# Second projection: VectorE and ScalarE kept in program order, and other PSUM banks for its first block

## The chip, the cores and the metric

The kernel runs on one core of a Trainium2 chip. The metric is the device time of one execution in microseconds. Five engines work beside each other, each through its own queue of instructions: TensorE (matmuls, PE in the profile, its weight loads PEld), VectorE (DVE), ScalarE (ACT), GpSimd (POOL) and SyncE (SP, which here issues nearly all loads).

## The reference

One layer of a decoder trunk on a sequence of 1024 rows of width 1024, everything in float32. What matters here is its end:

```
y_b = rms_norm(yz, ssm_norm_w ...)            # SSM branch, 2048 wide, normed in 8 groups
merged = sigmoid(g_a) * (y_a @ w_proj_a) + sigmoid(g_b) * (y_b @ w_proj_b)
x + gate * (merged @ w_out)                   # and a final rms_norm
```

`y_a @ w_proj_a` is called the first projection in this text, `y_b @ w_proj_b` the second, `merged @ w_out` the output product.

## The kernel before, in words

**Stages.** The kernel multiplies the normed input by a wide weight matrix, runs the SSD scan, and fills TensorE's gaps in the scan with the first projection (`proj_a`, eight blocks of 128 output columns, each accumulated in two PSUM banks, `pma`). L1308 empties those two banks with the gate applied and a store writes the result to DRAM. Then come the second projection (L1401 to L1647) and the output product (L1711 to L1778).

**Precision and operands.** A float32 product is made of three matmuls: an operand is split into a high part (a ScalarE cast, L1455, L1460, L1515, L1558) and a low part (a VectorE subtraction of the high part from the original, L1456, L1461, L1516, L1559), and high x high, high x low and low x high are added up in PSUM.

**The second projection.** It is a two-by-two product of blocks done with seven block products in place of eight (a Strassen form): p1, p5, p2, p3, p6, p7, p4 in this order. Each has eight steps `k`, numbered through as 56 units `u`. One step is twelve matmuls of 128x128 by 128x512, three into each of four PSUM banks (`multiply`, L1470). There are two sets of four banks: `psx` (tiles `x`), used by p1, p6, p7, p4, and `psy` (tiles `yp`), used by p5, p2, p3. p6, p7 and p4 add onto what p1 left in `psx`.

**What a step does.** In the loop at L1593, unit `u` issues its matmuls, then (`ahead`, L1570) the loads of unit u+6 (`loads`) and the operands of unit u+4 (`operands`, L1437). Operands are: for the four products that meet a fresh block of y, a norm on VectorE (`y_norm`, L1416); for p5, p6 and p7 a subtraction of blocks (L1447, L1449, L1452); the cast and the low part into rings of five slots (L1455, L1456); for p1 and p2 the cast and the low part of the weight block too (L1460, L1461); for p6 one more subtraction (L1463). In p1, two row sums of squares (`post2`, `post3`: TensorE, L1117 and L1131 on VectorE, L1121 on GpSimd, a store on ScalarE's queue) are finished for the last two groups of the norm. In the odd steps of p3, p7 and p4 a result is `merged` (L1521): gate times sum plus the other branch (L1527, L1528), and the sums that the output product needs (L1536 to L1542, and a split after a11). In p4 the splits of w_out begin (`BESIDE`). At the last step of a block its four banks are emptied: p1 and p5 by ScalarE copies (L1627, L1633), p2, p3, p6 and p7 by VectorE additions (L1630, L1637, L1640, L1643), p4 by `merged`.

**What sets the order.** The kernel is written in a layer that chooses the order of each engine's queue when it is compiled: it takes instructions by priority as a built-in model of the time says they are ready. `pin` (`keep_in_program_order`, L78) ties an instruction behind the one traced just before it on the same engine, so that it can't be moved ahead. `tc.high_priority()` lets an instruction be taken early. Before the change, all matmuls and all loads are pinned. On VectorE and ScalarE in the second projection only the splits of the first four units are, and the two L1308 of the last block of the first projection; the rest is ordered by the compiler's model. Each queue is then worked through in the order in which it was compiled.

**Banks.** `banks` (L1369) takes four PSUM banks for a set. Before, `psy` is taken first and so gets the lower four banks, `psx` the upper four.

Of the kernel before, what the change touches and what calls it, by code (L numbers as in the profile page):

```python
# [8 lines left out]
F32 = mybir.dt.float32  # L9
# [3 lines left out]
ALU = mybir.AluOpType  # L13
# [3 lines left out]
P = 128  # L17
# [18 lines left out]
def hybrid_kernel(  # L36
# [7 lines left out]
    V, A, G, PE = nc.vector, nc.scalar, nc.gpsimd, nc.tensor  # L44
# [33 lines left out]
    pin = tc.keep_in_program_order  # L78
# [7 lines left out]
    def f32(t):  # L86
        return t.bitcast(F32)
# [41 lines left out]
    snw = par2[:, 32:48]  # L129
# [38 lines left out]
    with tc.tile_pool(name="p0", bufs=1, reuse_waits="tile") as p0:  # L168
# [261 lines left out]
        sums = {(7, 5): [(last_sums, 0)], (7, 6): [(last_sums, 1)], (7, 8): [(last_sums, 2)]}  # L430
# [935 lines left out]
    room.extend(tag for k in range(KT - 2) for tag in ya_tags[k])  # L1366
    draw(left[0] - 5)

    def banks(name, c):  # L1369
        return [psb.tile([P, 512], F32, name=f"{name}{j}", tag=f"b{c}{j}") for j in range(4)]  # L1370

    big_r = [0]

# [30 lines left out]
    yt, rbs = {}, {}  # L1404
# [8 lines left out]

    def y_norm(n, h):
        t = yt[n, h]
        V.scalar_tensor_tensor(t, t, snw[:, n : n + 1], rbs[n // 2, h], op0=ALU.mult, op1=ALU.mult)  # L1416

    units = [(nm, k) for nm in ("p1", "p5", "p2", "p3", "p6", "p7", "p4") for k in range(KT)]
    aops, bops, raws = {}, {}, {}
# [17 lines left out]
    def operands(u):  # L1437

        nm, k = units[u]
        if nm in fresh:  # L1440
            n, h = fresh[nm]
            y_norm(n + k, h)
        b11, b12 = yt[k, 0], yt.get((k, 1))
        b21, b22 = yt.get((KT + k, 0)), yt.get((KT + k, 1))
        t = {"p1": b11, "p2": b21, "p5": b12, "p3": b22, "p6": b12, "p7": b11, "p4": b21}[nm]
        if nm == "p5":
            V.tensor_sub(b12, b12, b11)  # L1447
        elif nm == "p6":
            V.tensor_sub(b12, b22, b12)  # L1449
            give(f"yn{KT + k}_1")  # L1450
        elif nm == "p7":
            V.tensor_sub(b11, b12, b11)  # L1452
        hi, lo = turn(bh_r, f"{nm}bh{k}"), turn(bl_r, f"{nm}bl{k}")
        keep = pin if u < 4 else lambda i: i
        keep(A.copy(hi, t))  # L1455
        keep(V.tensor_sub(lo, t, f32(hi)))  # L1456
        bops[u] = hi, lo
        if nm not in WB:
            a, raw = aops[u], raws.pop(u)
            keep(A.copy(a[:, 0], raw))  # L1460
            keep(V.tensor_sub(a[:, 1], raw, f32(a[:, 0])))  # L1461
        if nm == "p6":
            V.tensor_sub(b21, b21, b12)  # L1463
        elif nm == "p7":
            give(f"yn{k}_0")
            give(f"yn{k}_1")
        elif nm == "p4":
            give(f"yn{KT + k}_0")

    def multiply(u, ps):  # L1470
        nm, k = units[u]
        first = nm in ("p1", "p5", "p2", "p3")
        a, (bh, bl) = aops.pop(u), bops.pop(u)
        for j in range(4):
            js = slice(j * P, (j + 1) * P)
            for n, (v, r) in enumerate(((0, bh), (0, bl), (1, bh))):
                pin(PE.matmul(ps[j], a[:, v, js], r, start=first and n + k == 0, stop=n == 2 and k == KT - 1,  # L1477
                              skip_group_check=not first))
# [30 lines left out]
    raw, opa, opb, freed = {}, {}, {}, {}  # L1509

    def split(nm, j, last=True):

        t, name = raw.pop((nm, j)) if last else raw[nm, j]
        hi, lo = place(f"{nm}h{j}"), place(f"{nm}l{j}")
        A.copy(hi[0], t)  # L1515
        V.tensor_sub(lo[0], t, f32(hi[0]))  # L1516
        opa[nm, j], freed[nm, j] = (hi[0], lo[0]), [hi, lo]
        if last and name:
            give(name)

    def merged(b, h, c, name):  # L1521


        th, ma = gates.pop((b, h))
        j, dst = b % 4, th if c is None else c
        acc = psx[j] if c is None else c
        V.scalar_tensor_tensor(dst, th, 1.0, acc, op0=ALU.add, op1=ALU.mult)  # L1527
        V.tensor_add(dst, dst, ma)  # L1528
        nm = (("a11", "a21"), ("a12", "a22"))[b // 4][h]
        raw[nm, j] = dst, name  # L1530
        if nm == "a11":
            split(nm, j, False)
        elif nm == "a21":
            raw["s3", j] = raw.pop(("a11", j))
            s3 = raw["s3", j][0]
            V.tensor_sub(s3, s3, dst)  # L1536
        elif nm == "a22":
            raw["s1", j] = raw.pop(("a21", j))
            s1, s3 = raw["s1", j][0], raw["s3", j][0]
            V.tensor_add(s1, s1, dst)  # L1540
            s2 = slot_tile(f"s2_{j}")
            V.tensor_sub(s2, dst, s3)  # L1542
            raw["s2", j] = s2, f"s2_{j}"

    def fourth(j):
        s4 = slot_tile(f"s4_{j}")
        V.tensor_sub(s4, raw["a12", j][0], raw["s2", j][0])
        raw["s4", j] = s4, f"s4_{j}"

    wor = {}  # L1550
# [4 lines left out]

    def wo_split(nm, j):
        hi, t = place(f"wh{nm}{j}"), wor.pop((nm, j))
        A.copy(hi[0], f32(t))  # L1558
        V.tensor_sub(t, f32(t), f32(hi[0]))  # L1559
        opb[nm, j] = [hi, (t, f"wl{nm}{j}")]  # L1560

    rows = {}
# [24 lines left out]
    psx = psy = None  # L1587
# [5 lines left out]
    for u, (nm, k) in enumerate(units):  # L1593
        if k == 0:
            if nm == "p1":
                psy = banks("yp5", "y")
                psx = banks("x", "x")
                rows_bank[0] = lambda name: psy[("pr6", "pr7", "pq6_1", "pq7_1").index(name)]
            elif nm in ("p2", "p3"):
                psy = banks(f"y{nm}", "y")  # L1600
            elif nm == "p6":
                room.extend(rb_r[0])
            ps = psy if nm in ("p2", "p5", "p3") else psx
        multiply(u, ps)
        ahead(u)
        if nm == "p1" and k in (1, 4):
            late = groups[NG - 2 + k // 4]
            late.post2(1, late.late)
        if nm == "p1" and k == 4:
            for tags, _ in (y1_r, ym_r):  # L1610
                room.extend(tags)
        if nm == "p1" and k in (4, 6):
            groups[NG - 4 + k // 2].post3()
        if k % 2 and nm in GATES:
            gate_load(GATES[nm][0] + k // 2, GATES[nm][1])
        if nm == "p4":
            for at, f, a in BESIDE:
                if at == k:
                    f(*a)
        if k % 2 and more and nm not in ("p2", "p5"):  # L1620
            merged(*more.pop(0))
        if k == KT - 1:
            for j in range(4):
                with tc.high_priority():
                    if nm == "p1":
                        t = slot_tile(f"c11_{j}")
                        A.copy(t, psx[j])  # L1627
                        more.append((j, 0, t, f"c11_{j}"))
                    elif nm == "p2":
                        V.tensor_add(more[j][2], more[j][2], psy[j])  # L1630
                    elif nm == "p5":
                        t = slot_tile(f"p5_{j}")
                        A.copy(t, psy[j])  # L1633
                        sums.append(t)
                    elif nm == "p3":
                        t = slot_tile(f"p3_{j}")
                        V.tensor_add(t, sums[j], psy[j])  # L1637
                        sums.append(t)
                    elif nm == "p6":
                        V.tensor_add(sums[4 + j], sums[4 + j], psx[j])  # L1640
                        more.append((j, 1, sums[4 + j], f"p3_{j}"))
                    elif nm == "p7":
                        V.tensor_add(sums[j], sums[j], psx[j])  # L1643
# [75 lines left out]
    acc = {"x": banks("ox", "y"), "y": banks("oy", "x")}  # L1719
# [54 lines left out]
    y = inv_root(3, 1, dde[:, 33:34])  # L1774
# [38 lines left out]
```

## Time and profile before

| | |
|---|---|
| runs of the kernel before | 1404.32, 1408.84, 1409.13 us; median 1408.84 |
| the profiled execution | 1407.67 us |
| its span, first to last instruction | 1405.9 us |
| granted TensorE clock, mean | 0.997 |
| second projection, first matmul | 1156.92 us from the span's start |
| output product, first matmul | 1320.6 us |

Times in the timelines are microseconds from the start of the span. A timeline row gives start, duration, engine, source line, operation, output and inputs, size, count, and in brackets how long the engine sat idle before it and who released it. A window row gives its length, then the busy time and number of instructions of PE, PEld, DVE, ACT and POOL, then the granted TensorE clock, the share of the DMA engines in use, and GB/s. Matmuls overlap at their ends, so one of 0.39 us follows the next after 0.227.

### The profile page before, as it was taken

Reading aid. Unit: us, or ns where it says so; the run is one execution under the profiler, and the core shown is the slowest. Engines: PE = TensorE matmul, PEld = TensorE weight load, DVE = VectorE, ACT = ScalarE, POOL = GpSimd, SP = SyncE. Lnnn points to the kernel's source line nnn. Section 1 sums busy time; section 2 is a strip of 40 time slices with the busy share of each in tenths; the row PEclk is TensorE's granted clock in tenths of the full one; section 3 lists DMA queues with packets and bytes.
Section 4 is the critical chain, followed back from the end, with each engine's and each line's share of the span. In section 5 each row is a group of like instructions: output and inputs, shape, how many; then the busy total and the mean of one; then the engine's idle time right before and its main releaser. Section 6 shows DMA issues by size and latency. Waiting matters only on the chain.

```text
span 1405.9 us, 20633 instructions
## 1 busy us (share of the span) xinstructions
PE 1377.1 (98%) x7035; PEld 1139.9 (81%) x7035; DVE 1062.4 (76%) x1863; ACT 797.0 (57%) x1471; POOL 213.0 (15%) x208
## 2 busy tenths in 40 slices
PE   8999999999999999999999999999999999999997
PEld 6688888888888888888887888888888877878886
DVE  4786776777778889889788796388667767876976
ACT  5764576556656665556565555677766723322443
POOL 0000000000000011111000010038778740000001
PEclk9999999999999999999999999999999999999999
DMA  8653343343344777787675774598778749878903
GB/s 263 173 165 98 113 120 105 105 121 120 116 125 134 214 202 239 236 248 232 192 221 156 240 214 135 173 353 318 262 253 296 275 168 328 320 231 296 350 33 120
DMA packets 273150, 283.37 MB, mean 202 GB/s; under 512 B 15341, under 2 KB 223637, under 8 KB 273045
## 3 DMA queue, kind: packets, MB, share of 16 engines
q1 hardware_dynamic: 185684, 198.52, 44.4%
q10 hardware_dynamic: 87360, 83.54, 17.8%
q8 instruction: 55, 0.90, 0.3%
q14 instruction: 51, 0.41, 0.1%
HBM read 194.55 MB, written 87.46 MB: 201 GB/s over the span
## 4 chain that ended last, share of the span: by engine, by line
PE 80%; DMA 8%; DVE 5%; POOL 2%; issue 2%; ACT 1%; SPq 1%; ACTq 0%; DVEq 0%; POOLq 0%
PE xcb L574 6%; PE xuz L574 6%; PE xz L574 6%; PE xx L574 5%; PE xg L574 5%; PE x L1477 4%; PE yp L1477 4%; PE ox L1676 3%; PE yuz L574 3%; PE ycb L574 3%; PE pma L81 3%; PE xv L574 3%; PE yz L574 3%; PE yg L574 3%; PE yx L574 3%; DMA dcy<-acs_d 3%
## 5 line engine op out<-in xcount | busy, mean ns | idle before, releaser
L793 POOL TENSOR_TENSOR wog<-wog,gb 128x256 f32<-128x256 f32 x16 | 18.3, 1159 | 676.6 <-PE zz L574 413.3
L1007 ACT ACTIVATE dcy<-dcy,nacs 128x128 f32<-128x128 f32 x256 | 78.6, 388 | 14.9 <-POOL dcy L1002 14.5
L1002 POOL TENSOR_SCALAR_AFFINE_SELECT dcy<-dcy 128x1024 f32<-128x1024 f32 x32 | 35.0, 1095 | 135.7 <-ACT ea L999 132.3
L999 ACT ACTIVATE ea<-dcy 64x512 f32<-64x512 f32 x64 | 40.1, 626 | 14.2 <-DMA dcy<-acs_d 13.8
L920 ACT ACTIVATE ac<-ac 128x1024 f32<-128x1024 f32 x32 | 33.9, 1060 | 23.0 <-DVE ac L918 22.8
L81 PE MATMUL pma<-yh,wah 128*128 128x512 f32 x128 | 43.3, 419 | 0.0
L1027 DVE TENSOR_TENSOR dcy<-dcy,pc 128x1024 f32<-128x1024 f32 x32 | 39.0, 1218 | 4.8 <-PE pc L84 3.0
L81 PE MATMUL pma<-yh,wal 128*128 128x512 f32 x128 | 42.5, 413 | 0.0
L1089 POOL TENSOR_TENSOR yz<-y,sl 128x512 f32<-128x512 f32 x32 | 41.4, 1295 | 1.1
L1087 DVE TENSOR_TENSOR ym<-yn,ea 128x512 f32<-128x512 f32 (+1 forms) x32 | 19.9, 622 | 28.5 <-PE yn L81 28.3
L81 PE MATMUL pma<-yl,wah 128*128 128x512 f32 x128 | 40.1, 394 | 0.0
L1088 POOL TENSOR_TENSOR y<-y,ym 128x512 f32<-128x512 f32 (+1 forms) x32 | 36.6, 1144 | 14.4 <-DVE ym L1087 14.4
L81 PEld LDWEIGHTS yn<-sl,st 128*128 128x128 f32 x224 | 30.3, 190 | 8.3 <-issue 4.4
L81 PE MATMUL yn<-sl,st 128*128 128x128 f32 x224 | 31.6, 276 | 4.9 <-DVE st L1057 4.9
L1416 DVE SCALAR_TENSOR_TENSOR yn<-yn,par,rb 128x512 f32<-128x512 f32 x32 | 24.0, 749 | 15.7 <-DMA yn<-yb_d 15.5
L81 PE MATMUL sp<-xe,bn 128*128 128x256 f32 x112 | 32.6, 408 | 3.3 <-DVE ssq L1117 1.7
L81 PE MATMUL yi<-dcy,xd 128*64 128x128 f32 x512 | 35.7, 283 | 0.0
L918 DVE SCALAR_TENSOR_TENSOR ac<-c2x,cwt,ac 128x1023 f32<-128x1023 f32 (+2 forms) x24 | 31.2, 1300 | 5.3 <-ACT ac L916 5.1
L918 DVE SCALAR_TENSOR_TENSOR ac<-c2cb,cwt,ac 128x1023 f32<-128x1023 f32 (+2 forms) x24 | 31.1, 1296 | 4.4 <-ACT ac L916 4.3
L1691 POOL TENSOR_TENSOR r<-r,fnw 128x512 f32<-128x512 f32 x2 | 2.5, 1296 | 203.7 <-DMA out_dram<-r 203.7
L1055 POOL TENSOR_TENSOR st<-st,cd 128x256 f32<-128x256 f32 x48 | 32.1, 668 | 8.0 <-PE yn L81 5.3
L918 DVE SCALAR_TENSOR_TENSOR ac<-c1cb,cwt,ac 128x1023 f32<-128x1023 f32 (+2 forms) x24 | 31.6, 1318 | 1.3 <-ACT ac L916 1.3
(2980 smaller groups left out, 4390.9 us busy)
## 6 DMA issues: line engine op xcount, KB each, us to landing
sl<-s_d SPq DMA_DIRECT2D x32, 768.0 KB
s_d<-ac ACTq DMA_DIRECT2D x32, 512.0 KB
dcy<-acs_d SPq DMA_DIRECT2D x32, 512.0 KB
aw<-in_ada_w_dram SPq DMA_DIRECT2D x16, 512.0 KB
wbr<-in_w_proj_b_dram SPq DMA_DIRECT2D x64, 128.0 KB
wb_d<-wbb ACTq DMA_DIRECT2D x32, 256.0 KB
wb_d<-wbc ACTq DMA_DIRECT2D x32, 256.0 KB
yb_d<-yz ACTq DMA_DIRECT2D x32, 256.0 KB
```

The source lines that it names most:

```text
L81: pin(PE.matmul(acc, l, r, start=first, stop=last))
L574: pin(PE.matmul(ps, lw[:, k * P : (k + 1) * P], r[k], start=first and n + k == 0, stop=n == 2 and k == 3, skip_group_check=not first))
L918: V.scalar_tensor_tensor(ac[:, s:], cc[:, : S - s], conv_wt[:, 3 - s, i : i + 1], ac[:, s:], op0=ALU.mult, op1=ALU.add)
L920: A.activation(ac, ac, AF.Silu)
L999: A.activation(ea[hh * HD : (hh + 1) * HD], dcy.rearrange("p (j e) i l -> p e j (i l)", e=2)[hh * HD : (hh + 1) * HD, hh], AF.Exp)
L1002: G.affine_select(out=d8, in_=d8, compare_op=ALU.is_ge, fill=-1e30, base=0, pattern=[[0, 2 * HPG], [1, P]], channel_multiplier=-1)
L1007: A.activation(dcy[:, h, i, :], dcy[:, h, i, :], AF.Exp, bias=sub[:, i, h : h + 1])
L1027: V.tensor_tensor(d3, d3, pc[:, 0:256].unsqueeze(1).to_broadcast([P, HPG, 256]), op=ALU.mult)
L1088: G.tensor_add(y1[:, :, t0:], y1[:, :, t0:], m[:, :, t0:])
L1089: G.tensor_mul(yz, y1, sl[:, 4:6])
L1477: pin(PE.matmul(ps[j], a[:, v, js], r, start=first and n + k == 0, stop=n == 2 and k == KT - 1, skip_group_check=not first))
L1676: pin(PE.matmul(ps, a[:, tsl], b[:, cs], start=first and n + j == 0, stop=n == 2 and j == 3, skip_group_check=not first))
```

## The change

Every VectorE and ScalarE instruction of the second projection is pinned: norms, subtractions, casts, low parts, `merged`, the emptying of the banks, and, up to its end, the splits of w_out. In the output product the splits of its left operands and the sums s4 are pinned too, while the emptying of its banks, the squares and the splits of w_out there are not. And the first allocation of banks takes three banks for `psy`, then the four of `psx`, then the fourth of `psy`, so that `psx` moves down by one bank. The diff, without repeats of the same edit:

```diff
-    def banks(name, c):
-        return [psb.tile([P, 512], F32, name=f"{name}{j}", tag=f"b{c}{j}") for j in range(4)]
+    def banks(name, c, n=4):
+        return [psb.tile([P, 512], F32, name=f"{name}{j}", tag=f"b{c}{j}") for j in range(n)]
...
-        V.scalar_tensor_tensor(t, t, snw[:, n : n + 1], rbs[n // 2, h], op0=ALU.mult, op1=ALU.mult)
+        pin(V.scalar_tensor_tensor(t, t, snw[:, n : n + 1], rbs[n // 2, h], op0=ALU.mult, op1=ALU.mult))
...
-            V.tensor_sub(b12, b12, b11)
+            pin(V.tensor_sub(b12, b12, b11))
...
-        keep = pin if u < 4 else lambda i: i
-        keep(A.copy(hi, t))
-        keep(V.tensor_sub(lo, t, f32(hi)))
+        pin(A.copy(hi, t))
+        pin(V.tensor_sub(lo, t, f32(hi)))
...
-        A.copy(hi[0], t)
-        V.tensor_sub(lo[0], t, f32(hi[0]))
+        pin(A.copy(hi[0], t))
+        pin(V.tensor_sub(lo[0], t, f32(hi[0])))
...
-        V.scalar_tensor_tensor(dst, th, 1.0, acc, op0=ALU.add, op1=ALU.mult)
-        V.tensor_add(dst, dst, ma)
+        pin(V.scalar_tensor_tensor(dst, th, 1.0, acc, op0=ALU.add, op1=ALU.mult))
+        pin(V.tensor_add(dst, dst, ma))
...
-        A.copy(hi[0], f32(t))
-        V.tensor_sub(t, f32(t), f32(hi[0]))
+        keep = pin if psx is not None and not acc else lambda i: i
+        keep(A.copy(hi[0], f32(t)))
+        keep(V.tensor_sub(t, f32(t), f32(hi[0])))
...
-                psy = banks("yp5", "y")
+                psy = banks("yp5", "y", 3)
                 psx = banks("x", "x")
+                psy += [psb.tile([P, 512], F32, name="yp53", tag="by3")]
...
-                        V.tensor_add(more[j][2], more[j][2], psy[j])
+                        pin(V.tensor_add(more[j][2], more[j][2], psy[j]))
...
-                        V.tensor_add(sums[4 + j], sums[4 + j], psx[j])
+                        pin(V.tensor_add(sums[4 + j], sums[4 + j], psx[j]))
```

More of the change, by code (lines that the diff above doesn't have):

```diff
@@ L1459, in operands @@
             a, raw = aops[u], raws.pop(u)
-            keep(A.copy(a[:, 0], raw))
-            keep(V.tensor_sub(a[:, 1], raw, f32(a[:, 0])))
+            pin(A.copy(a[:, 0], raw))
+            pin(V.tensor_sub(a[:, 1], raw, f32(a[:, 0])))
         if nm == "p6":
-            V.tensor_sub(b21, b21, b12)
+            pin(V.tensor_sub(b21, b21, b12))
         elif nm == "p7":
@@ L1535, in merged @@
             s3 = raw["s3", j][0]
-            V.tensor_sub(s3, s3, dst)
+            pin(V.tensor_sub(s3, s3, dst))
         elif nm == "a22":
@@ L1539, in merged @@
             s1, s3 = raw["s1", j][0], raw["s3", j][0]
-            V.tensor_add(s1, s1, dst)
+            pin(V.tensor_add(s1, s1, dst))
             s2 = slot_tile(f"s2_{j}")
-            V.tensor_sub(s2, dst, s3)
+            pin(V.tensor_sub(s2, dst, s3))
             raw["s2", j] = s2, f"s2_{j}"
@@ L1546, in fourth @@
         s4 = slot_tile(f"s4_{j}")
-        V.tensor_sub(s4, raw["a12", j][0], raw["s2", j][0])
+        pin(V.tensor_sub(s4, raw["a12", j][0], raw["s2", j][0]))
         raw["s4", j] = s4, f"s4_{j}"
@@ L1586, in hybrid_kernel @@
     psb = ps3.__enter__()
-    psx = psy = None
+    psx = psy = acc = None
     sums, more = [], []
@@ L1626, in hybrid_kernel @@
                         t = slot_tile(f"c11_{j}")
-                        A.copy(t, psx[j])
+                        pin(A.copy(t, psx[j]))
                         more.append((j, 0, t, f"c11_{j}"))
                     elif nm == "p2":
-                        V.tensor_add(more[j][2], more[j][2], psy[j])
+                        pin(V.tensor_add(more[j][2], more[j][2], psy[j]))
                     elif nm == "p5":
                         t = slot_tile(f"p5_{j}")
-                        A.copy(t, psy[j])
+                        pin(A.copy(t, psy[j]))
                         sums.append(t)
@@ L1636, in hybrid_kernel @@
                         t = slot_tile(f"p3_{j}")
-                        V.tensor_add(t, sums[j], psy[j])
+                        pin(V.tensor_add(t, sums[j], psy[j]))
                         sums.append(t)
                     elif nm == "p6":
-                        V.tensor_add(sums[4 + j], sums[4 + j], psx[j])
+                        pin(V.tensor_add(sums[4 + j], sums[4 + j], psx[j]))
                         more.append((j, 1, sums[4 + j], f"p3_{j}"))
                     elif nm == "p7":
-                        V.tensor_add(sums[j], sums[j], psx[j])
+                        pin(V.tensor_add(sums[j], sums[j], psx[j]))
                         more.append((4 + j, 1, sums[j], f"p5_{j}"))
```

4 lines of the change are left out of this document (2 added, 2 removed).

## The prediction

> **What bounds the kernel now.** The page first:
>
> ```profile
> PE 1377.1 (98%) x7035; PEld 1139.9 (81%) x7035; DVE 1062.4 (76%) x1863; ACT 797.0 (57%) x1471; POOL 213.0 (15%) x208
> ...
> PE 80%; DMA 8%; DVE 5%; POOL 2%; issue 2%; ACT 1%; SPq 1%; ACTq 0%; DVEq 0%; POOLq 0%
> ```
>
> TensorE is busy for 98% of the span and carries 80% of the chain that ended last, so time can only be won where it idles. The windows, one for each block of the second projection (p1, p5, p2, p3, p6, p7, p4) and one for the output product, show where:
>
> ```profile
> core 0: us, PE busy (x) PEld busy (x) DVE busy (x) ACT busy (x) POOL busy (x), PEclk, DMA share, GB/s
> 1156.90:1186.10 29.20, 26.10 (x132) 21.48 (x131) 21.70 (x37) 9.28 (x16) 3.29 (x2) 1.00 0.87 307
> 1186.10:1207.90 21.80, 21.80 (x98) 18.06 (x97) 19.29 (x30) 12.53 (x22) 0.00 (x0) 1.00 0.89 331
> 1207.90:1230.40 22.50, 21.87 (x97) 17.81 (x96) 18.88 (x31) 6.59 (x12) 0.00 (x0) 1.00 0.93 336
> 1230.40:1254.40 24.00, 22.70 (x96) 17.87 (x97) 21.79 (x37) 6.81 (x12) 0.00 (x0) 1.00 0.63 202
> 1254.40:1276.20 21.80, 21.80 (x98) 18.02 (x97) 7.88 (x14) 4.99 (x8) 0.00 (x0) 1.00 0.85 293
> 1276.20:1298.10 21.90, 21.90 (x98) 17.97 (x97) 14.82 (x26) 5.66 (x10) 0.00 (x0) 1.00 0.87 310
> 1298.10:1320.60 22.50, 22.26 (x98) 18.00 (x97) 19.47 (x34) 6.06 (x11) 0.00 (x0) 1.00 0.83 304
> 1320.60:1395.50 74.90, 74.90 (x338) 62.27 (x338) 58.61 (x103) 35.34 (x75) 3.65 (x4) 1.00 0.34 129
> ```
>
> A block that never waits takes 21.8 us, 2.72 for each of its eight steps. Seven make 152.6; the projection takes 163.7. TensorE's timeline names most of the 11.1 us between:
>
> ```profile
> 1160.54 0.50 PE L1477 MATMUL x<-p1bh,p1a 128*128 128x512 f32 x1 [1.41 <-DVE tha L1308]
> ...
> 1164.07 1.84 PE L81 MATMUL yp<-ones,sq 128*128 128x1 f32 x16
> 1165.77 0.49 PE L1477 MATMUL x<-p1bh,p1a 128*128 128x512 f32 x1
> ...
> 1183.21 0.27 PE L84 MATMUL yp<-ident,ssq 128*8 128x128 f32 x1 [1.69 <-POOL ssq L1121]
> ...
> 1230.41 0.47 PE L1477 MATMUL yp<-p3bh,p3a 128*128 128x512 f32 x1 [0.64 <-issue]
> ...
> 1233.36 0.50 PE L1477 MATMUL yp<-p3bh,p3a 128*128 128x512 f32 x1 [0.84 <-DVE c L1630]
> ```
>
> p1 waits for L1308 to empty a bank of the first projection, does two groups of sixteen row sums (1.70 each, real work), and waits for a factor that GpSimd makes from VectorE's L1117. p3 waits for banks that VectorE (L1630) empties late.
>
> **The change, part by part.** No instruction or DMA is added. What changes is VectorE's and ScalarE's order, and four banks.
>
> *The price of strict order.* The two engines hand each operand back and forth. The rows, VectorE's and then ScalarE's:
>
> ```profile
> 1150.38 0.15 DVE L1117 TENSOR_SCALAR ssq<-pq 128x4 f32<-128x4 f32 x1
> ...
> 1154.61 0.75 DVE L1416 SCALAR_TENSOR_TENSOR yn<-yn,par,rb 128x512 f32<-128x512 f32 x1 [1.58 <-DMA yn<-yb_d]
> ...
> 1159.81 1.28 DVE L1308 SCALAR_TENSOR_TENSOR tha<-tha,pma 128x512 f32<-128x512 f32 x2
> ...
> 1181.27 0.15 DVE L1117 TENSOR_SCALAR ssq<-yp 128x4 f32<-128x4 f32 x1
> ...
> 1227.82 0.69 DVE L1463 TENSOR_TENSOR yn<-yn,yn 128x512 f32<-128x512 f32 x1
> 1228.42 0.69 DVE L1452 TENSOR_TENSOR yn<-yn,yn 128x512 f32<-128x512 f32 x1
> ...
> 1239.36 0.69 DVE L1528 TENSOR_TENSOR c<-c,ma 128x512 f32<-128x512 f32 x1
> ...
> 1263.45 0.69 DVE L1456 TENSOR_TENSOR p6bl<-yn,p6bh 128x512 fp32r<-128x512 f32 x1 [2.03 <-ACT p6bh L1455]
> ```
>
> ```profile
> 1155.39 0.62 ACT L1455 CAST p1bh<-yn 128x512 fp32r<-128x512 f32 x1 [3.70 <-DVE yn L1416]
> 1155.91 0.62 ACT L1460 CAST p1a<-p1r 128x512 fp32r<-128x512 f32 x1
> ...
> 1206.01 2.63 ACT L1633 COPY p<-yp 128x512 f32<-128x512 f32 x4
> ...
> 1240.08 0.62 ACT L1515 CAST ma11h<-c 128x512 fp32r<-128x512 f32 x1 [0.59 <-DVE c L1528]
> ...
> 1262.79 0.62 ACT L1455 CAST p6bh<-yn 128x512 fp32r<-128x512 f32 x1 [2.10 <-PE x L1477]
> ```
>
> From a y_norm to the cast that reads it 0.78; from another VectorE operation to its reader 0.72; from a cast to its low part 0.66; between independent operations 0.60. Before, VectorE fills the gap with work of other steps; in program order it stands. One step's operands then take VectorE: p1 and p2 0.78+0.66+0.60+0.60 = 2.64; p5, with a subtraction, 0.78+0.72+0.66+0.60 = 2.76; p3 2.04; p6 (subtract, low part, subtract) 0.72+0.66+0.60+0.60 = 2.58; p7 1.98. A `merged` with its split (a11, in p3) takes 0.72+0.72+0.66+0.60 = 2.70, one in p7 (a21) 2.04. In a step the program has the operands of the step four further on, then `merged`, and in a block's last step the emptying of the banks. So behind each waiting low part stand all later operands and the banks, for which TensorE waits. Up to p7's start there are 48 such handovers (40 steps, four a11, four of p7): if each were off by 0.05, the queue would end 2.4 earlier or later, which bounds this estimate at both ends.
>
> *p1.* The new banks should free p1 of L1308: none of its other three banks waited, so L1308's second bank lies outside them. With L1117 no longer behind later operands the wait for GpSimd goes too: VectorE reaches it near 1176, behind p5's first operands; from the L1117 at 1181.27 to the factor's use at 1183.21 took 1.94, so it is there at 1178, and TensorE wants it near 1179. p1 becomes 21.8+3.4 = 25.2, and p5 starts at 1182.1 instead of 1186.1.
>
> *p5 to p2.* p2 needs p5's banks, emptied by ScalarE (L1633) behind the casts of p2's step 3, which wait for VectorE. VectorE's pinned row begins behind the L1117 at 1150.38: 8x2.64, two L1308 1.2, the four small L1117/L1131 0.6, 8x2.76, and 3x2.64+0.78 reach 1204.1; two casts (0.52 apart) and one copy (0.66) give 1206.0. TensorE is there at 1203.9: **2.1 lost**. p2 runs from 1206.1; its own banks are emptied in time (VectorE has 0.9 us in hand), so p3 starts at 1227.9, 2.5 ahead of before.
>
> *p3 and p6.* VectorE's queue from emptying p2's first bank to emptying p6's first: 4x0.60 (p2's banks), 4x2.04 (p3's last operands), 8x2.58 (p6), 4x2.70 (a11), 4x0.60 (p3's banks), 4x1.98 (p7's first) = 52.3 us. TensorE needs 43.6. With VectorE 0.9 ahead at the start and 0.7 for the last emptying, p7 starts at 1227.0+52.3+0.7 = 1280.0 instead of 1271.5: **8.5 lost**, about 2.4 in the middle of p6 for want of an operand and 6.1 in one piece at p7's start. Before, p7 starts at 1276.2.
>
> *The clock.* An idle stretch in the SSD stage shows what a long gap does:
>
> ```profile
> 1030.49 0.68 PE L81 MATMUL yn<-sl,st 128*128 128x128 f32 x4 [2.77 <-DVE st L1057]
> ```
>
> ```profile
> 1030.40:1033.90 3.50, 3.41 (x21) 3.09 (x23) 1.84 (x3) 1.53 (x4) 2.74 (x4) 0.62 0.95 330
> ```
>
> After 2.77 idle the granted clock averaged 0.62 over 3.5 us; after 1.41 and 1.69 (p1's window) it stayed 1.00. The 6.1 at p7 should cost (1-0.5)x3.4 = **1.7**, an estimate that takes the clock as halved there. The shorter gaps at p2 and in p6 lie between these rows; I count them as nothing (p6's is covered by VectorE's queue anyway), and keep 1.7 for p2's as a rival. [...]
>
> *p7 to p4.* In p7's last step the fourth a21 now stands ahead of emptying the banks: 0.2 (cast behind the step before, an estimate)+0.66+0.60+2.04+0.72 = 4.2 against 2.72: **1.5 lost**. p7 takes 21.8+1.7, so p4 starts at 1305.0 and ends at 1326.8, **6.2** behind 1320.6.
>
> *p4 and SP's queue.* In p4 four a22 (0.72+0.72+0.60+0.60 = 2.64 each) and the splits of w_out take turns with TensorE's own pace, and the pinned emptying ends about 5 us into the output product, whose second part, the first to need those banks, starts 10.9 in (four by four by three matmuls of 0.227): nothing lost, and 5.9 of cover left. SP's order is unchanged, but a gate load waits until `merged` has let go of its slot; that is later now by VectorE's lag, up to 8 us, against the six steps (16 us) that operand loads run ahead. I count nothing for it.
>
> *Output product.* The splits of a22, s4 and a12 are now pinned behind the squares of L1689.
>
> ```profile
> 1355.99 0.69 DVE L1687 TENSOR_TENSOR r<-r,ox 128x512 f32<-128x512 f32 x1 [0.40 <-PE ox L1676]
> ```
>
> ```profile
> 1356.71 0.63 ACT L1689 ACTIVATE junk<-r 128x512 f32<-128x512 f32 x1 [2.30 <-DVE r L1687]
> ...
> 1362.93 0.63 ACT L1689 ACTIVATE junk<-r 128x512 f32<-128x512 f32 x1
> 1363.46 0.19 ACT L1689 ACTIVATION_READ_ACCUMULATOR junk<-r 128x1 f32 x1
> 1363.56 0.60 ACT L1558 CAST ms1h<-wlb 128x512 fp32r<-128x512 f32 x1
> ```
>
> Add to square 0.72, square to cast 0.63, cast to low part 0.66, low part 0.69: 2.7 behind a product's end. The next product uses it in its twelfth matmul, 2.5 in: 0.2 to 0.3 at three borders, **0.8**. Bounds: nothing, or the whole 2.7 at one border.
>
> Sum: 6.2+0.8 = +7.0. The profiled execution took 1407.67 (span 1405.9, 1.8 around it): **1414.7 us**. It lies between the runs shown, 1.2 under their median of 1408.84.
>
> **The rivals.** *Faster:* VectorE is not late. In p3 and p6 it has only 21.79+7.88 = 29.7 us of work. Of the 52.3, twenty handovers are idle, about 0.8 each; below 0.36 each, it fits into 43.6, and the gains stand alone: p1 4.0, p2 and p3 2.9, p4 0.7, less 0.8: 1400.9. For it: pins tie an instruction only to the one traced before it, and loose ones give freedom. Against: hardly any is left loose. *The bank does not do what it says:* if the new banks hold L1308's second one, p1 starts at 1162.3; p5 and p2 follow 5.4 later, less the 2.1 wait: +3.2, 1417.9. *Another clock drop*, at p2: 1416.4. *Loads in line:* a late yn now holds the banks too.
>
> ```profile
> L1416 DVE SCALAR_TENSOR_TENSOR yn<-yn,par,rb 128x512 f32<-128x512 f32 x31 | 23.2, 750 | 15.7 <-DMA yn<-yb_d 15.5
> ```
>
> VectorE waited 15.5 for them in all. I count none, since each is in before its turn by the times above; one or two waits of 3 would give 1418 to 1421.
>
> **How the numbers follow.** Forecast 0.48, faster 0.15, banks 0.04, clock 0.15, loads 0.18. What a measurement here can tell from no change is 0.5%, about 7.0 us, where the forecast itself lies. Slower by more: half the forecast, most of the last three: 0.57. Faster by more: half its rival, 0.07. The rest, 0.36, is within. Range 1403 to 1421: under it most of the faster rival, over it the worst of the loads.
>
> **What would show it.** No wait for L1308 in p1 and p5 near 1182; VectorE's low parts led by ACT casts in every step; a TensorE gap of about 2 at p2 (L1633) and about 6 at p7 (L1640), with a low clock behind it; p4 ending near 1327. If p7 starts without a wait, the queue sum is wrong, and with it the sign.

## The result, and the profile after

The changed kernel takes **1424.84 us** in the median of six runs (1417.82 to 1425.78); beside it the kernel before took 1408.99 (1404.32 to 1412.07, six runs). The ratio is 1.0115, with a 95% interval of 1.0097 to 1.0133: 1.2% slower. The prediction was 1414.7, in a range from 1403 to 1421. Its sign is right, and the time is above the range. The profiled execution took 1424.17 (span 1422.4), which is 16.5 more than the 1407.67 of the one before.

The page of the changed kernel, the chain that ended last by engine:

```profile
PE 74%; DMA 8%; DVE 8%; ACT 4%; issue 3%; POOL 2%; SPq 1%; ACTq 0%; DVEq 0%; POOLq 0%
```

TensorE's share of the chain fell from 80 to 74%, VectorE's rose from 5 to 8%, ScalarE's from 1 to 4%: TensorE now waits for the two engines whose order was fixed. The windows of the changed kernel, one for each block but p3 (21.80, without a wait) and one for the whole output product, show where:

```profile
1155.70:1181.30 25.60, 25.60 (x131) 21.63 (x130) 18.41 (x32) 9.23 (x17) 4.35 (x2) 1.00 0.89 314
1181.30:1206.60 25.30, 21.93 (x97) 17.84 (x95) 18.28 (x28) 10.11 (x19) 0.00 (x0) 1.00 0.92 322
1206.60:1230.10 23.50, 23.46 (x96) 19.28 (x97) 14.63 (x23) 8.40 (x15) 0.00 (x0) 0.93 0.86 302
...
1251.90:1283.30 31.40, 23.94 (x97) 18.79 (x96) 22.36 (x37) 7.44 (x12) 0.00 (x0) 0.93 0.60 208
1283.30:1309.50 26.20, 24.72 (x97) 19.88 (x97) 18.18 (x29) 5.58 (x9) 0.00 (x0) 0.89 0.55 189
1309.50:1331.40 21.90, 21.90 (x97) 18.10 (x98) 19.21 (x31) 5.29 (x9) 0.00 (x0) 1.00 0.86 288
...
1331.40:1413.40 82.00, 78.98 (x349) 62.92 (x347) 64.36 (x108) 35.61 (x78) 4.37 (x5) 1.00 0.38 145
```

To the end of TensorE's work, the output product of the kernel before is this window:

```profile
1320.40:1396.90 76.50, 76.50 (x349) 63.63 (x347) 60.21 (x106) 36.13 (x77) 3.94 (x5) 1.00 0.33 127
```

So the projection went from 163.5 us (1156.9 to 1320.4) to 175.7, **12.2 more**, and the output product from 76.5 to 82.0, **5.5 more**. p1 began 1.2 earlier; together 16.5. In the projection, p5 (25.3 with the wait behind it), p2 (23.5 at a clock of 0.93), p6 (31.4 up to p7's start) and p7 (26.2 at 0.89) lose. Waits are only part of it: p2 and p7 are also longer while TensorE is busy.

TensorE's timeline in the changed kernel: its waits over 0.4 us from p1 to the end, and one of 0.30 that follows another at the same border:

```profile
1206.64 0.50 PE L1476 MATMUL yp<-p2bh,p2a 128*128 128x512 f32 x1 [3.41 <-ACT p L1634]
...
1265.13 0.80 PE L1476 MATMUL x<-p6bh,p6a 128*128 128x512 f32 x1 [2.18 <-ACT p6bh L1454]
...
1283.31 0.77 PE L1476 MATMUL x<-p7bh,p7a 128*128 128x512 f32 x1 [5.29 <-issue]
...
1309.49 0.47 PE L1476 MATMUL x<-p4bh,p4a 128*128 128x512 f32 x1 [1.47 <-ACT p4bh L1454]
...
1377.62 0.50 PE L1677 MATMUL ox<-ma11h 128*128 128x512 f32 x1 [0.46 <-ACT ma11h L1514]
...
1378.66 0.50 PE L1677 MATMUL ox<-ma11h,ma11h 128*128 128x512 f32 x1 [0.30 <-DVE ma11h L1515]
...
1389.80 0.50 PE L1677 MATMUL oy<-ms1h,mwhb 128*128 128x512 f32 x1 [0.42 <-ACT mwhb L1514]
...
1402.88 0.50 PE L1677 MATMUL oy<-whb,a12l 128*128 128x512 f32 x1 [0.68 <-DVE a12l L1515]
1404.57 0.50 PE L1677 MATMUL oy<-ms1h,mwhb 128*128 128x512 f32 x1 [0.72 <-DVE mwhb L1515]
```

All four waits of before are gone: L1308, GpSimd's factor and the two of p3. Four larger ones stand in the projection, and small ones at the borders between the products of the output product. (The line numbers have moved by one: the casts and low parts of the operands are L1454 and L1455, the multiply L1476, the emptying of p2, p5, p3 and p6 L1631, L1634, L1638 and L1641.) The 5.29 at p7 has no releaser's name; VectorE's timeline gives it. The bracket is the engine's idle time before a row:

```profile
1228.94 2.48 DVE L1631 TENSOR_TENSOR c<-c,yp 128x512 f32<-128x512 f32 x4
...
1246.67 0.69 DVE L1455 TENSOR_TENSOR p6bl<-yn,p6bh 128x512 fp32r<-128x512 f32 x1 [0.76 <-ACT p6bh L1454]
1247.28 0.69 DVE L1462 TENSOR_TENSOR yn<-yn,yn 128x512 f32<-128x512 f32 x1
...
1249.33 0.69 DVE L1455 TENSOR_TENSOR p6bl<-yn,p6bh 128x512 fp32r<-128x512 f32 x1 [0.77 <-ACT p6bh L1454]
...
1282.53 2.48 DVE L1641 TENSOR_TENSOR p<-p,x 128x512 f32<-128x512 f32 x4
```

A step of p6 is a subtraction, an idle 0.76 for ScalarE's cast, the low part, a subtraction. From the emptying of p2's first bank (1228.94) to that of p6's first bank (1282.53), which p7 needs, lie 53.6 us; p7 starts 0.78 later. The row of VectorE's waits for p6 (us in total, times, longest):

```profile
DVE p6bl L1455 <- ACT p6bh L1454: 6.1, 8, 0.8
```

VectorE waits in each of the block's eight steps. For a load of yn it waits nowhere in the projection any more (before: 15.5 us in all, over the span).

### The profile page after: what moved, and what is told of

It is laid out like the page before. It is cut to its first block, busy times and chain, and to the rows that moved or that the text cites. A ratio compares the mean times of both kernels' runs of the same rounds, so it can differ in the third digit from the quotient of the medians.

```text
span 1422.4 us, 20633 instructions
## 1 busy us (share of the span) xinstructions
PE 1383.4 (97%) x7035; PEld 1144.0 (80%) x7035; DVE 1067.5 (75%) x1863; ACT 793.2 (56%) x1471; POOL 216.6 (15%) x208
## 4 chain that ended last, share of the span: by engine, by line
PE 74%; DMA 8%; DVE 8%; ACT 4%; issue 3%; POOL 2%; SPq 1%; ACTq 0%; DVEq 0%; POOLq 0%
PE xx L574 6%; PE xz L574 6%; PE xuz L574 6%; PE xcb L574 5%; PE xg L574 5%; PE x L1476 3%; PE pma L81 3%; PE xv L574 3%; PE yx L574 3%; PE ox L1677 3%; PE yuz L574 3%; PE ycb L574 3%; PE yg L574 3%; PE yz L574 3%; DMA dcy<-acs_d 3%
## 5 line engine op out<-in xcount | busy, mean ns | idle before, releaser
L1007 ACT ACTIVATE dcy<-dcy,nacs 128x128 f32<-128x128 f32 x256 | 78.6, 388 | 15.5 <-POOL dcy L1002 14.9
L81 PEld LDWEIGHTS yi<-dcy,xd 128*64 128x64 f32 x512 | 28.0, 139 | 4.5 <-issue 2.4
```

Source lines behind the costliest of these rows:

```text
L81: pin(PE.matmul(acc, l, r, start=first, stop=last))
L1007: A.activation(dcy[:, h, i, :], dcy[:, h, i, :], AF.Exp, bias=sub[:, i, h : h + 1])
```

## The experiments

The theory: **in strict order VectorE stands idle for each cast of ScalarE; its queue becomes longer than TensorE's time, and most of TensorE's longer idle stretches are followed by a low clock (in the changed kernel 0.53 to 0.56 over 3.4 to 6.7 us at those of 3.41, 2.18 and 5.29, and 1.00 behind that of 1.47); in the output product the pinned splits come late.** Rivals: the other banks are to blame; a fixed order costs time whatever the order is; the emptying of the banks merely stands in the wrong place of its step.

Until some 20 us ahead of p1 all these programs do the same, and yet p1 starts between 1153.4 and 1160.9 in their profiled executions. So whole times tell 2 us apart only in many runs, and the stages are compared by their own lengths. Each kernel has one trace, and it is not always of a typical execution: it took 1428.94 where the median is 1422.79 (old banks), 1411.64 against 1409.59 (inputs ahead), 1416.75 against 1420.31 (splits free), and 1399.38 and 1400.12 against 1402.75 and 1401.09 (the last two kernels).

### The banks alone

```diff
-                psy = banks("yp5", "y")
+                psy = banks("yp5", "y", 3)
                 psx = banks("x", "x")
+                psy += [psb.tile([P, 512], F32, name="yp53", tag="by3")]
```

This is put into the kernel before, without the new pins.

> The kernel before with the other banks alone, nothing pinned in addition. My theory (the fixed order of VectorE and ScalarE is what costs time, and the other banks only take away p1's wait of 1.41 us for L1308): 1 to 1.5 us less than before, about 1407.5, which 3 rounds can hardly tell from no change; p1's first wait is gone. Rival (the other banks are what costs the 15.9 us between the two kernels, for example because they now wait for another reader): above 1415.

Measured: 1406.26 us (1404.59 to 1409.07, 10 runs), ratio 0.9995 (0.9981 to 1.0008). The window of its projection:

```profile
1156.40:1318.50 162.10, 157.92 (x708) 129.15 (x707) 123.32 (x199) 51.17 (x87) 3.28 (x2) 1.00 0.85 300
```

162.1 against 163.5, and no wait for L1308: the banks do what they say and are worth about that wait of 1.41. They cost nothing. The rival that blames them falls.

### The old banks in the changed kernel

```diff
-                psy = banks("yp5", "y", 3)
+                psy = banks("yp5", "y")
                 psx = banks("x", "x")
-                psy += [psb.tile([P, 512], F32, name="yp53", tag="by3")]
```

> The changed kernel with the old banks, so that p1 again waits for L1308. My theory: VectorE reaches L1308 only behind the pinned row of operands, so p1 waits some 4 to 5 us at its second or third multiply; p1 and p5 come later by that, but p2 and p7 wait for VectorE anyway, so that nearly all of it is given back there: 0 to 3 us above the changed kernel, 1424 to 1428. Rival (the other banks are to blame): back towards 1409.

Measured: 1422.79 us (1422.21 to 1428.94, 4 runs), ratio 1.0117 (1.0086 to 1.0148). TensorE's waits in p1 and ahead of p2:

```profile
1165.61 0.50 PE L1476 MATMUL x<-p1bh,p1a 128*128 128x512 f32 x1 [2.50 <-DVE tha L1308]
...
1214.02 0.50 PE L1476 MATMUL yp<-p2bh,p2a 128*128 128x512 f32 x1 [1.20 <-ACT p L1633]
```

p1 waits 2.50, where 4 to 5 were expected, and has a low clock (0.94 in the mean of the block, 1.00 in the changed kernel); it takes 30.0 (1160.9 to 1190.9) instead of 25.6. The projection is nevertheless 175.2 long (1160.9 to 1336.1), about as in the changed kernel: p2's wait shrinks from 3.41 to 1.20, p2 itself from 23.5 to 21.9 without a low clock behind it (1.00 in the mean of p2, where it was 0.93), and p7 with the wait behind it from 26.2 to 25.1. What the other banks win in p1 is lost again from p2 on. The expected time of 1424 to 1428 was a little high; the ratio cannot be told from the changed kernel's.

### The inputs of a cast one step ahead

```diff
-    def operands(u):
+    def inputs(u):
...
         elif nm == "p7":
             pin(V.tensor_sub(b11, b12, b11))
+
+    def operands(u):
...
+        if u + LEAD + 1 < len(units):
+            inputs(u + LEAD + 1)
         if u + LEAD < len(units):
             operands(u + LEAD)
```

All instructions stay, and stay pinned; only what a cast reads is traced ahead of the former step's cast and low part.

> The changed kernel, with the fixed order kept, but each step's y_norm or subtraction (what the cast reads) is traced one step earlier, ahead of the former step's cast and low part. So VectorE has work that does not depend on the cast while the cast runs, with the same instructions in all. My theory (what makes VectorE late is that it stands about 0.76 us in each step for ScalarE's cast): 40 steps win up to 0.7 us each, the waits of 3.41 at p2, 2.18 in p6 and 5.29 at p7 go, and with them the low clock; p4 keeps its 1.5; the projection ends near 1314 in place of 1331.4, the output product stays near 80.6, the time is about 1406. Rival (a fixed order costs the time whatever the order is, since VectorE can no longer pass a wait): the waits stay and the time is about 1424. If one of the two is only part of it, p7's wait shrinks by part.

Measured: 1409.59 us (1406.89 to 1413.18, 10 runs), ratio 1.0010 (0.9995 to 1.0025). VectorE's timeline in p6's operands:

```profile
1243.33 0.68 DVE L1448 TENSOR_TENSOR yn<-yn,yn 128x512 f32<-128x512 f32 x1
1243.93 0.69 DVE L1461 TENSOR_TENSOR p6bl<-yn,p6bh 128x512 fp32r<-128x512 f32 x1
1244.53 0.69 DVE L1468 TENSOR_TENSOR yn<-yn,yn 128x512 f32<-128x512 f32 x1
```

The same three instructions, now 0.60 apart with no idle time: 1.8 for a step that took 2.66 (1246.67 to 1249.33). The windows of its projection and of its output product:

```profile
1156.10:1317.90 161.80, 158.40 (x708) 130.76 (x707) 125.13 (x200) 49.80 (x87) 4.92 (x2) 0.99 0.84 286
1317.90:1400.90 83.00, 80.42 (x349) 63.77 (x347) 64.29 (x108) 35.61 (x78) 4.37 (x5) 0.98 0.38 144
```

The projection lost 13.9 us, from 175.7 to 161.8, and the waits at p2, in p6 and at p7 are gone. The output product stays long; its 83.0 hold a stretch of low clock, from 1389.78 on (3.41 us at 0.50), that the changed kernel's 82.0 do not (1.00 in the mean). So it is not the fixed order that costs the time in the projection, but the idle place that it leaves beside each cast. The expected 1406 was missed by 3.6. TensorE's timeline shows a new wait in p5:

```profile
1184.55 0.50 PE L1482 MATMUL yp<-p5bh,p5a 128*128 128x512 f32 x1 [1.98 <-DVE tri L1131]
```

The copy of the last row sums (L1131) now stands behind a low part that waits 2.75 us for its cast, and p5 takes 25.7 instead of 21.8: the 1.98 and a low clock (0.57 from 1184.50 to 1187.90). The order alone does not explain it. In the kernel with both edits, which has the same order here, that low part waits 2.73 too, yet it comes 2.7 sooner after p1's start, and p5 does not wait. For the five loads of yn before it VectorE waited 7.1 us in all here, and 3.6 there. So the wait goes with late loads in the traced execution; how many of the ten executions had it is not shown.

### The output product's splits free

```diff
-        pin(A.copy(hi[0], t))
-        pin(V.tensor_sub(lo[0], t, f32(hi[0])))
+        keep = pin if not acc else lambda i: i
+        keep(A.copy(hi[0], t))
+        keep(V.tensor_sub(lo[0], t, f32(hi[0])))
...
-        pin(V.tensor_sub(s4, raw["a12", j][0], raw["s2", j][0]))
+        V.tensor_sub(s4, raw["a12", j][0], raw["s2", j][0])
```

> The changed kernel, but what split and fourth trace during the output product is left unpinned; in the projection all stays pinned. My theory (the output product lost 5.7 us because the splits of a22, s4 and a12 stand in VectorE's line behind the additions into banks and the wide multiplies of L1700): the output product goes from 80.6 back to about 75, and the time to about 1419; p7 still starts near 1283. Rival (the output product is longer because the projection hands its operands over later): it stays at 80 to 81, and the time at about 1424.

Measured: 1420.31 us (1416.75 to 1422.64, 4 runs), ratio 1.0087 (1.0058 to 1.0116). Its output product:

```profile
1329.50:1406.00 76.50, 76.49 (x349) 63.63 (x347) 61.45 (x108) 35.82 (x77) 3.96 (x5) 1.00 0.41 156
```

76.5, the length of before, behind a projection as long as the changed kernel's (176.1). (The expectation counted the output product to 1412.0 in the changed kernel and to 1395.5 in the one before, hence its 80.6 and 75.) The 5.5 us of the output product come from the pins of `split` and `fourth` and not from the projection's lag.

### The wide multiplies behind a12's splits

```diff
-            V.scalar_tensor_tensor(r, r, y, fnw, op0=ALU.mult, op1=ALU.mult)
+            pin(V.scalar_tensor_tensor(r, r, y, fnw, op0=ALU.mult, op1=ALU.mult))
...
             if nm == "a12":
+                for i in (4 + t, 7)[: 2 - min(t, 1)]:
+                    finish(i, y4[:, i - 4 : i - 3])
                 finish(t, root(t))
...
-            if nm == "s4":
-                finish(4 + t, y4[:, t : t + 1])
```

> The changed kernel with its pins, but the four wide multiplies of L1700 that finish the rows of s4 (1.28 and 3.67 us of VectorE's time, ahead of three additions into banks) are traced in a12's own steps and pinned there, behind the splits of a12. My theory (the border from s4 to a12 loses its 2.65 us because these multiplies hold up the additions, behind which the squares and the pinned splits stand): the waits of 0.40, 0.68 and 0.72 near the end shrink below 0.3 each, and the output product goes from 82.0 to about 79.5, while the waits of 0.46, 0.30 and 0.42 at the two earlier borders stay. Rival (every pinned split costs the same, whatever stands ahead of it): 82, with the late waits as they were. The time changes by 2 to 3, which these rounds will hardly show.

Measured: 1425.35 us (1423.48 to 1428.92, 4 runs), ratio 1.0108 (1.0073 to 1.0142). Ten us at the border from s4 to a12 hold 32 matmuls in the changed kernel:

```profile
1397.00:1407.00 10.00, 8.19 (x32) 5.35 (x32) 7.68 (x10) 4.22 (x11) 2.98 (x2) 1.00 0.38 152
```

and here 37, in the same ten us from the start of the output product (1.8 later), with an output product of 81.4:

```profile
1398.80:1408.80 10.00, 8.62 (x37) 6.52 (x36) 6.70 (x8) 3.19 (x8) 2.56 (x2) 1.00 0.01 2
1333.20:1414.60 81.40, 78.73 (x349) 63.01 (x347) 62.21 (x106) 35.29 (x76) 3.63 (x4) 1.00 0.35 135
```

Five matmuls of 0.227 are 1.1 us at this border, of which 0.6 is left in the whole product; the rest is lost at 1346.58 and 1358.00, in products that the edit does not touch. Two waits remain, 0.67 and 0.71, where the theory wanted less than 0.3. So **this reading of mine falls for the most part**: L1700 holds about a third of what this border costs (3.1 us, see below), and the other two borders are as they were. What is common to the three borders is the rest. With the pins, the last split of an operand stands behind the square of the same block's last product. In the changed kernel, at the border from s3 to a22, ScalarE does the square first:

```profile
1376.34 0.63 ACT L1690 ACTIVATE junk<-r 128x512 f32<-128x512 f32 x1
...
1376.97 0.60 ACT L1514 CAST ma11h<-p 128x512 fp32r<-128x512 f32 x1
```

With the splits free, the same cast (at 1370.97) stands ahead of that square (1375.76), with one more square between:

```profile
1370.97 0.62 ACT L1515 CAST ma11h<-p 128x512 fp32r<-128x512 f32 x1 [1.67 <-PE ox L1678]
...
1375.76 0.63 ACT L1691 ACTIVATE junk<-r 128x512 f32<-128x512 f32 x1
```

### The emptying first

```diff
         multiply(u, ps)
+        if nm not in ("p1", "p4") and k == KT - 1:
+            for j in range(4):
...
         ahead(u)
```

The loop that empties the banks of p5, p2, p3, p6 and p7 moves, as it is, from the end of the step to this place.

> The changed kernel, with the emptying of the banks of p5, p2, p3, p6 and p7 traced ahead of the operands and the merged of the same step; the number of VectorE's instructions and of its waits for ScalarE stays. My theory (VectorE's queue as a whole is too long): p2's wait shrinks by one step's operands of 2.64 and p4's of 1.47 goes, but from p2's banks to p6's lies as much work as before, 53.6 us, so that p7 still waits 4 to 7; p7 starts near 1280, the time is 1418 to 1421. Rival (VectorE is in time, and only the place of the emptying behind other work of its step is bad): p7's wait falls below 1, and the time to 1413 or less.

Measured: 1422.42 us (1419.80 to 1423.45, 4 runs), ratio 1.0104 (1.0081 to 1.0127). TensorE's waits in its projection, and the window of the projection:

```profile
1209.75 0.50 PE L1476 MATMUL yp<-p2bh,p2a 128*128 128x512 f32 x1 [1.37 <-ACT p L1614]
...
1263.07 0.50 PE L1476 MATMUL x<-p6bh,p6a 128*128 128x512 f32 x1 [1.30 <-ACT p6bh L1454]
...
1284.55 0.59 PE L1476 MATMUL x<-p7bh,p7a 128*128 128x512 f32 x1 [4.40 <-issue]
```

```profile
1160.90:1329.80 168.90, 161.12 (x708) 131.66 (x707) 125.08 (x196) 50.87 (x88) 4.35 (x2) 0.98 0.79 269
```

VectorE's two ends of the queue, p2's first bank and p6's:

```profile
1230.13 2.47 DVE L1611 TENSOR_TENSOR c<-c,yp 128x512 f32<-128x512 f32 x4
...
1283.77 2.48 DVE L1621 TENSOR_TENSOR p<-p,x 128x512 f32<-128x512 f32 x4
```

p4's wait is gone and p2's is 2.0 shorter; but between the two emptyings lie 53.6 us as before, and p7 still waits 4.40. The place of the emptying counts at p2 and p4; at p7 it is the length of the queue. The projection is 6.8 shorter than the changed kernel's. That the whole time shows only some 2 of it, 1422.4 where at most 1421 was expected, goes with p1's start: 1160.9 instead of 1155.7 in the profiled execution, behind a program that is the same up to there; when p1 started in the other executions is not shown.

### TensorE kept at work in p7's gap

```diff
+                fill_y = psb.tile([P, 512], F32, name="fill", tag="by0")
...
+        if nm == "p7" and k == 0:
+            for _ in range(16):
+                mm(fill_y[:, 0:P], ident, ones)
         multiply(u, ps)
```

> The changed kernel with 16 more matmuls (128x128 into a bank that nobody reads) between p6 and p7, some 4.4 us of work that fills most of p7's wait of 5.29. p7 starts where it did, near 1283. If the low clock after the wait costs time on its own, p7's 24.7 us go back towards 21.8 and the time falls by 2 to 3, to about 1421. If it does not, p7 keeps its 24.7 and the time stays at about 1424. If the added matmuls are in the way of p7's own, the time is over 1425.

Measured: 1422.71 us (1421.80 to 1424.35, 4 runs), ratio 1.0109 (1.0084 to 1.0135). TensorE's timeline at p7's start (the 16 matmuls leave 32 records), and p7's window:

```profile
1279.70 3.73 PE L81 MATMUL fill<-ones,ident 128*128 128x128 f32 x32
1285.11 0.47 PE L1476 MATMUL x<-p7bh,p7a 128*128 128x512 f32 x1 [1.68 <-issue]
```

```profile
1285.10:1308.60 23.50, 22.02 (x96) 17.94 (x97) 18.13 (x29) 5.59 (x9) 0.00 (x0) 1.00 0.59 199
```

p7 ran at a clock of 1.00 and was busy for 22.0 instead of 24.7: **the low clock behind the gap costs 2.7 us on its own**, though p7 still started when VectorE let it. The whole time differs by less than these runs tell apart.

### Both edits that gain, and two waits less

The first kernel is the inputs ahead together with the free splits:

> Both edits that gained, together: each step's y_norm or subtraction one step ahead of its cast, and the splits of the output product unpinned. If the two losses are separate, as my theory has it (handovers in the projection, splits behind VectorE's wide work in the output product), their gains add: 1409.6 of the first less some 6 for the output product (83.0 back to 76.5 by its trace), about 1403.5. Rival (the output product takes up slack that the projection left, so that the gains overlap): 1407 or more.

The second has two more lines moved:

```diff
         if u + LEAD + 1 < len(units):
             inputs(u + LEAD + 1)
+        if units[u] == ("p1", 6):
+            groups[NG - 1].post3()
         if u + LEAD < len(units):
             operands(u + LEAD)
...
-        if k % 2 and more and nm not in ("p2", "p5"):
+        held = nm == "p7" and k == KT - 1
+        if k % 2 and more and nm not in ("p2", "p5") and not held:
             merged(*more.pop(0))
...
+            if held:
+                merged(*more.pop(0))
```

> As the kernel with both edits, and two more lines moved for the two waits that its projection still has: the copy of the last row of sums (L1131) is traced ahead of the operands whose cast waits for a buffer, and in p7's last step the fourth merged comes behind the emptying of the banks. p5's wait of 1.98 with its low clock (25.7 in place of 21.8) and p4's of 1.43 should go: 3.9 and 1.4 less than that kernel, about 1398 to 1400, 0.6% under the kernel before. Rival (the low clock in p5 and the waits only move to the next block): 1402 or more.

Measured: **1402.75 us** (1399.38 to 1405.81, 10 runs), ratio 0.9964 (0.9951 to 0.9977), and **1401.09 us** (1400.12 to 1404.11, 8 runs), ratio 0.9958 (0.9943 to 0.9974). Both beat the kernel before, by 0.4%. The first one's projection and output product:

```profile
1154.30:1312.10 157.80, 156.38 (x707) 129.63 (x706) 123.66 (x197) 49.67 (x86) 4.92 (x2) 1.00 0.85 293
...
1312.10:1388.60 76.50, 76.50 (x349) 63.66 (x348) 61.37 (x108) 35.83 (x77) 3.92 (x5) 1.00 0.41 156
```

and the second one's:

```profile
1155.60:1311.70 156.10, 156.10 (x707) 129.72 (x706) 122.46 (x195) 50.48 (x87) 4.92 (x2) 1.00 0.84 292
...
1311.70:1389.40 77.70, 76.80 (x349) 63.56 (x347) 63.72 (x112) 35.85 (x77) 3.99 (x5) 1.00 0.43 164
```

The two gains add, as expected. In the first one p5's wait is already gone without being moved (p5 is 21.7 there), so the second had less to win than was expected: 1.7 in the projection, of which the output product gave back 1.2. Its 1401.09 lies between what the two theories expected, and the two kernels cannot be told apart. In the second, TensorE is busy for all of the 156.1 us: seven blocks of 21.8 and two groups of row sums of 1.7 are 156.0. Nothing is left to win in the projection by ordering.

## Why the prediction was right in sign and wrong in size

Lengths from p1's own start, predicted and in the profile of the changed kernel:

| | predicted | measured |
|---|---|---|
| p1 | 25.2 | 25.6 |
| p5 up to p2's start | 24.0 | 25.3 |
| p2 to p7's start | 73.9 | 76.7 |
| p7 up to p4's start | 25.0 | 26.2 |
| p4 | 21.8 | 21.9 |
| output product, against before | +0.8 | +5.5 |

The projection was 5.8 short (169.9 against 175.7), the output product 4.7; p1's start gave 1.2 back. That is the 9.3 between +7.0 and the +16.5 of the profiled executions, but for 0.2 of rounding.

**Right:** no wait for L1308 and none for GpSimd, p1 at 25.6; the price of a step in VectorE's queue, handover by handover (p6: 2.58 predicted, 2.66 measured); that VectorE needs some ten us more than TensorE's 43.6 for the stretch up to p7 (52.3 predicted, 53.6 measured), with p7's start named as the largest gap; a wait in the middle of p6 (2.4 against 2.18) and one of 1.5 at p4 (1.47).

**The queue was sized a little small:** 52.3 against 53.6. The stretch has twenty of the 48 handovers, so each took 0.065 more than counted (a step of p6 2.66 instead of 2.58, one of p3 2.12 instead of 2.04), where the bound beside it allowed 0.05. p2's wait was 1.3 longer, and it was 3.95 to 4.41 in three other kernels with the same projection. On VectorE's row a low part of p5 stood 1.99 for its cast instead of 0.76 (at 1178.31; the trace puts ScalarE's delay, 3.70 idle ahead of the cast at 1177.65, down to a load of p5a, and a store of row sums stands just ahead of the cast in its queue). It recurs there, with 1.98 to 2.91, but was not tried by itself.

**The clock term failed.** "The shorter gaps at p2 and in p6 lie between these rows; I count them as nothing", and 1.7 for p7's gap. The 1.7, (1-0.5)x3.4, is the price of one stretch like the one that the kernel before shows behind its idle 2.77, 3.41 us at 0.50:

```profile
1031.25:1034.66 3.41, 3.41 (x25) 3.08 (x25) 2.56 (x4) 1.12 (x4) 2.68 (x3) 0.50 0.88 355
```

Three windows of the changed kernel behind its gaps show the drop:

```profile
1206.70:1210.10 3.40, 3.40 (x9) 2.70 (x10) 2.38 (x5) 2.38 (x5) 0.00 (x0) 0.55 1.01 386
1264.70:1268.10 3.40, 2.97 (x6) 2.11 (x7) 2.23 (x4) 1.00 (x2) 0.00 (x0) 0.56 0.43 169
1281.80:1288.50 6.70, 5.19 (x12) 4.13 (x13) 4.98 (x8) 0.70 (x2) 0.00 (x0) 0.53 0.00 0
```

It comes behind all three. At p2 it costs 1.7 (23.5 against 21.8), and since it delays p2's first bank (VectorE empties it 22.3 after p2's start, where 20.9 was predicted), most of it goes on through VectorE's queue to p7: ScalarE's casts in p2 wait for TensorE's multiplies (2.25 and 1.60 at 1211.33 and 1214.08). The kernel with the old banks bears this out: without the drop VectorE emptied that bank 20.7 after p2's start, and p7 started 75.1 behind p2 instead of 76.7. p6's drop was covered, as the prediction said: with the splits free it did not come (1.00 from 1263.4 to 1270.0), and p7 started 76.4 behind p2. Behind p7's gap it lasts twice as long (6.83 us at 0.50 instead of 3.41) and costs 2.7 (24.7 against 22.0) where 1.7 was counted. "Another clock drop, at p2" stood among the rivals, with a chance of 0.15 and at 1416.4; it came, together with the forecast.

**The output product's term failed most:** 0.8 against 5.5. The mechanism was named rightly (a split behind the square of the product before it), and its price was not. Counted as what TensorE's matmuls fall behind their pace of 0.227, the borders behind s3, a22 and s4 cost 1.3, 1.0 and 3.1 us, where 0.2 to 0.3 each was predicted; the last is more than the 2.7 given as the upper bound for all. The 2.7 us were set against the twelfth matmul alone, but the cast's own result is already needed by the tenth, so that the first two borders lose twice: 0.7 each at the tenth (1377.62, 1389.80), 0.6 and 0.3 at the twelfth (1378.66, 1390.56). At the last border several splits of a12 are late and not only the last one. VectorE and ScalarE also had other work in that chain, such as the splits of w_out, and the wide L1700 at the last border; and behind each wait TensorE's first matmul takes 0.50 and not 0.39. Of these only L1700's share was tried: 1.1 at its border.

**The rivals.** "Faster" is dead: the handovers idle 0.76 each, far over the 0.36 that it needed. "Loads in line" is dead, since VectorE waits for no yn. The banks did what they say. The range ended at 1421, the price of the worst rival. Of the rivals only the clock drop came; what carried the time over the range is the forecast's own term for the output product, whose error of 4.7 no rival stood for.

What stays open: how much of the border costs is due to the square ahead of each split and how much to the other work in the line.

## What to carry to other kernels

Where two engines hand an operand back and forth, as VectorE and ScalarE do here, fixing the order of the program can fix an idle place into each handover (0.76 us in p6's steps): count a step as the sum of its handovers and set it against the bound engine's pace. Then trace something independent between a cast and its reader before the order is fixed; here that alone took 13.9 us out of the projection. When a wait is predicted for TensorE, price the low clock behind it as well (1.7 and 2.7 us here), and at a border of products set each operand's chain against the first matmul that needs any part of it.

## What the runs showed of the hardware

In these runs the clock drops do not go by the length of a gap. Clock records of four kernels, from p1 to the end of the output product, start in us of the span, length, granted clock:

```
changed kernel:      1207.07 3.41 0.50;  1265.09 3.41 0.50;  1282.16 6.83 0.50
splits free:         1204.91 3.41 0.50;  1280.00 6.83 0.50
emptying first:      1264.27 3.41 0.50;  1284.75 3.41 0.50
inputs ahead:        1184.98 3.41 0.50;  1389.78 3.41 0.50
```

In each run the starts lie whole multiples of 3.413 us apart (58.02 is 17 of them, 17.07 is 5, 75.09 is 22, 20.48 is 6, 204.80 is 60), and a stretch is one or two of them long. The idle 2.18 in p6 drew a low stretch in the changed kernel and none in the kernel with the free splits:

```profile
1263.54 0.50 PE L1476 MATMUL x<-p6bh,p6a 128*128 128x512 f32 x1 [2.18 <-ACT p6bh L1454]
```

Low stretches also followed gaps of 1.30 (emptying first) and 1.98 (inputs ahead). In the changed kernel nearly the whole gap in p6 lies between two points of this grid (1261.68 and 1265.09, the first counted back from the second); with the free splits one of them (1262.93, counted back from 1280.00) falls into it. The idle time between two points does not settle it either. With the inputs ahead, waits of 0.41 and 0.67 between the point of 1389.78 and the one before it were followed by a low stretch; in the changed kernel 0.68 and 0.72 between two points (1401.63 and 1405.05, counted on from 1282.16) were not, nor with the splits free the 1.57 of the gap that lie ahead of 1262.93. What decides stays open.
